# One-hot products of the first expert pair in half tiles among the router's steps, and the first pair's order of work, in a hybrid retention / attention / MoE block

## The chip, the cores and the metric

The kernel runs on one core of a Trainium2 chip as one program. Times are device microseconds, from the first to the last instruction of an execution and a little around it; the metric is the median of several executions. One execution is taken with the hardware profiler, and all rows shown come from it.

## The reference

One decoder block on 512 tokens of width 1024, all float32:

```python
h = rms_norm(x, mix_norm_g);  z = h @ w_in                  # 1024 x 4864
y_r = (silu(rg) * group_norm(retention(rq, rk, rv))) @ w_ret_o
y_s = sliding_window_attention(rms(sq), rms(sk), sv) @ w_swa_o
x = x + (sigmoid(gate_r) * y_r + sigmoid(gate_s) * y_s) @ w_out
h = rms_norm(x, ffn_norm_g)
group = argmax(h @ w_rg + b_rg)                             # 4 groups
e1, e2 = top2(h @ w_re + b_re, inside the group)            # 8 experts in a group, 32 in all
x = x + sum over e1, e2 of  weight_e * (silu(h @ w_gate[e]) * (h @ w_up[e])) @ w_down[e]
x = x + sigmoid(rms_norm(x, ple_gate_norm_g) @ w_ple_gate) * rms_norm(p @ w_ple, ple_norm_g)
```

The experts' weights are 32 times 3 MB: gate and up together 2 MB, down 1 MB. They are read once.

## The kernel before

**Mixers.** Up to about 330 us the two mixers run. Then `wout(nh, t)` forms `x1 = x + merged @ w_out` for two halves of the columns and four token tiles t of 128, and the router's steps of tile t are laid among the products of later tiles by the lists `fill`.

**Router.** For a tile: `post_a` transposes x1 and sums its squares, `post_b` multiplies by the router's weights (bank 4), `post_t` is a chain of small VectorE steps that ends in the one-hot rows of the two chosen experts (L932 is its first one-hot sum), `post_c` counts each token's rank in its expert (TensorE, bank 6, L939; then `Rpf`, L944), `post_d` is a second chain of VectorE steps (weights of the two experts, one-hot row of the rank), `post_e` adds tokens and weights to the slot tables (TensorE, bank 7, L1008). `post_t` and `post_d` are generators: `turns(n)` sends n rounds of all that are open. Every engine works in the order in which the program names its instructions.

**Slots and pairs.** Each expert has 64 slots. Experts p and p + 16 form pair p, whose 128 slots are one tile. For pairs 1 to 15 the slots' tokens are fetched by an indirect DMA of GpSimd (`fetch`, L1053) from x1 in DRAM, with rows named by the table `toki`; TensorE turns them (`turn`, L1066) and VectorE multiplies by the norm's gain into `XG[p]` (`grow`, L951). Pair 0 has no fetch: `first(t)` forms the one-hot matrix `G0[t]` (L961) and multiplies x1 by it (L964, 16 products a tile), which sums to the turned tokens.

**A pair's work.** `gu` multiplies by gate and up (L1161, 32 products, the slots' weights freed after each half of the contraction), ScalarE takes silu (L1171) and VectorE multiplies (L1172); `ht` transposes twice (L1180) and copies (L1182); `down` has 16 products (L1203). Below pair 12 the result is scattered by token into the DRAM tensor `Y` (L1223). From pair 12 on, `combine` multiplies it by a one-hot matrix instead (L1232) and VectorE adds it to x2 (L1244, through three PSUM banks of the ring `gb`). `collect` reads Y back (L1444, eight reads of 0.5 MB) and `total` adds it (L1451, four adds after pair 13 and four after pair 14). `embed(t)` forms one tile of the per-layer embedding (L1263, then L1250 on ScalarE) at pairs 10 to 13. After pair 15 the tail (L1365 to L1424) follows.

**Weights.** SBUF is an arena of 101 units of 2 KB. A load of 1 MB takes a block of four units; there are 17 blocks for weights, and `AT` names a few places below unit 22 (`TZ`) for the first loads. `queue` lists all loads in a fixed order, for each pair gate/up (four loads) and then down (two); `pump` issues as many as there is room for on SyncE's queue (L315). `SyncE` also waits in order: a load waits until the last reader of its place is done. From pair 9 on, `KEEP` leaves units 46 to 73 out.

**Overflow.** `overflow()` treats experts with more than 64 tokens. It reads a count into registers of every engine and skips its body by a branch (`tc.If`, shown as L1280) when there is none, which is the case here. In the kernel before it stands in pair 0, between gate/up and the turning of pair 1.

Of the kernel before, what the change touches and what calls it, by code (L numbers as in the profile page):

```python
# [16 lines left out]
P = 128  # L17
# [167 lines left out]
def program(tc, I, out):  # L185
# [55 lines left out]
    AT = {("gu", 0, 0): 0, ("gu", 16, 0): 14, ("gu", 17, 1): 18}  # L241
# [51 lines left out]
    qi = [0]  # L293
# [584 lines left out]
    def post_a(t, hb):  # L878

        if hb == 0:  # L880
            XT[t] = (ar.get(4, at=4 + 2 * (t % 2)), small(2), small(1), small(1))
        xt, ss, ms, r = XT[t]
        xs = x1[t].f(1024)[:, hb * 512:(hb + 1) * 512]
        b = aux()
        for kk in range(4):
            T.transpose(b[:, kk * P:(kk + 1) * P], xs[:, kk * P:(kk + 1) * P], ident)
        A.activation(xt.f(2, 512)[:, hb, :], b, AF.Copy)
        A.activation(banks[5], xs, AF.Square, accum_out=ss[:, hb:hb + 1])

    def post_b(t, hb):  # L890
# [4 lines left out]
        if hb:  # L895
            xt.free()
# [61 lines left out]
    def first(t):  # L958

        g0 = G0[t].f(2, SLOTS)  # L960
        V.tensor_tensor(g0, C("io64")[:, None, :].to_broadcast([P, 2, SLOTS]),  # L961
                        Rpf[:, t, 0:2][:, :, None].to_broadcast([P, 2, SLOTS]), op=OP.is_equal)
        for k in range(8):
            T.matmul(banks[k // 4][:, (k % 4) * P:(k % 4 + 1) * P], x1[t].f(8, P)[:, k, :], G0[t].f(P),  # L964
                     start=(t == 0 and k % 4 == 0), stop=(t == 3), skip_group_check=True)
        if t == 3:
            XG[0] = ar.get(4, at=12)
            for hb in range(2):
                grow(hb, banks[hb], XG[0])
# [87 lines left out]
    def turn(p_, hb):  # L1057

        if p_ > 15:
            return  # L1060
        if hb == 0:
            XG[p_] = ar.get(4, at=12 + 2 * (p_ % 2))
        b = gb()
        for kk in range(4):
            k = hb * 4 + kk
            T.transpose(b[:, kk * P:(kk + 1) * P], XR[p_].f(8, P)[:, k, :], ident)  # L1066
        grow(hb, b, XG[p_])
        if hb:
            XR.pop(p_).free()
            fetch(p_ + 2)  # L1070
# [6 lines left out]
    es.enter_context(tc.manual_schedule(engines=MS))  # L1077
    for t in range(4):
# [11 lines left out]
    for t in range(4):  # L1090
# [27 lines left out]
        pump(1 if t == 3 else 0)  # L1118
    turns()
# [150 lines left out]
    def overflow():  # L1270

        gm, tb_, xg, h, th, o = (ar.get(kb, r=r, at=at) for kb, r, at in (
            (2, True, 1), (4, False, 2), (4, False, 8), (2, False, 4), (2, False, 5), (4, False, 6)))
        xr = ar.get(4, at=12)
        wb = [ar.get(8, at=14)] * 2
# [97 lines left out]
    tmain = Ring([1, 0, 6, 7])  # L1373
# [81 lines left out]
    for p_ in range(16):  # L1455
        if p_ in KEEP:
            ar.kept = set(range(*KEEP[p_]))
        if p_ == SC:
            collect()
        for lo in (0, 4):  # L1460
            pump(0)
            gu(p_, range(lo, lo + 4))
        pump(0)
        if p_ == 0:
            overflow()
            fetch(2)
        turn(p_ + 1, 0)
        turn(p_ + 1, 1)
# [8 lines left out]
        if p_ == SC - 1:  # L1477
            for i in range(8):
                V.tensor_scalar(io[:, i * SLOTS:(i + 1) * SLOTS], C("io64"), i * SLOTS - 1.0, None, op0=OP.add)
# [89 lines left out]
```

## Time and profile before

| what | value |
|---|---|
| median of 3 runs | 710.86 us (710.43 to 712.74) |
| the profiled execution's own time | 713.99 us |
| its span, first to last instruction | 712.2 us |
| TensorE busy | 657.6 us (92%) |
| VectorE, ScalarE, GpSimd busy | 45%, 28%, 9% |
| granted TensorE clock, mean | 0.977 |
| moved by DMA | 163.92 MB |

A line of the timeline gives start, duration, engine, source line, operation, out<-in, shape and count; instructions of a kind that follow each other are merged, so a merged line's duration runs from the first start to the last end. PE is TensorE, DVE VectorE, ACT ScalarE, POOL GpSimd, SP SyncE; a q behind the engine marks its sequencer. In square brackets stands how long the engine was idle before it and what ended that.

### The profile page before, as it was taken

To read this page: it belongs to the slowest core of one execution; us is meant where nothing else is said; L and a number is where in the kernel's file an instruction comes from. 1 tells how busy PE (TensorE), PEld (TensorE's weight loads), DVE (VectorE), ACT (ScalarE), POOL (GpSimd) and SP (SyncE) were. 2 spreads that over 40 slices of the span, in tenths; PEclk is the share of its full clock that TensorE was granted. 3 is DMA by queue.
4 is the path that set the end of the run, shared out by engine and by line. 5 is a ranking of instruction groups with operands and counts; after the bars stand their busy time and mean duration, and the time that the engine had idled before them with its cause. 6 is when DMAs were issued, how large, how long until landed. Compare 5 with 4: busy or idle time off the path is not lost. (4 is left out here: it accounts for less than half of the span.)

```text
span 712.2 us, 8327 instructions
## 1 busy us (share of the span) xinstructions
PE 657.6 (92%) x3194; PEld 447.5 (63%) x3194; DVE 317.1 (45%) x692; ACT 198.2 (28%) x390; POOL 66.9 (9%) x67
## 2 busy tenths in 40 slices
PE   7999999999999999999988498998878889898997
PEld 6868887878888888888884243333323334334786
DVE  5485545842466156442362112112112234677753
ACT  6654243543334334230420000000001111006231
POOL 2013000000010000000000111111101121005100
PEclk9999999999999999999999799999999999999999
DMA  9727211340335420339891399999999989990011
GB/s 279 279 80 285 80 60 60 118 178 1 119 119 228 186 100 19 119 130 422 335 368 61 148 395 422 418 419 421 418 422 418 391 358 417 420 390 4 30 44 45
DMA packets 32474, 163.92 MB, mean 230 GB/s; under 512 B 5344, under 2 KB 8032, under 8 KB 16304
## 3 DMA queue, kind: packets, MB, share of 16 engines
q1 hardware_dynamic: 26672, 149.90, 53.2%
q0 software_dynamic: 5040, 11.35, 4.1%
q10 hardware_dynamic: 720, 2.11, 0.7%
q8 instruction: 26, 0.43, 0.3%
q14 instruction: 16, 0.13, 0.0%
HBM read 155.67 MB, written 14.68 MB: 239 GB/s over the span
## 5 line engine op out<-in xcount | busy, mean ns | idle before, releaser
L422 PE MATMUL bank<-slab,slab 128*128 128x512 f32 x320 | 126.4, 395 | 0.0
L423 PE MATMUL bank<-slab,slab 128*128 128x512 f32 x320 | 125.0, 391 | 0.0
L424 PE MATMUL bank<-slab,slab 128*128 128x512 f32 x320 | 124.8, 391 | 0.0
L1161 PE MATMUL bank<-slab,slab 128*64 128x512 f32 x512 | 118.7, 607 | 4.2 <-DMA slab<-wgu 4.2
L1161 PEld LDWEIGHTS bank<-slab,slab 128*64 128x64 f32 x512 | 43.5, 140 | 75.9 <-issue 67.7
L1203 PE MATMUL bank<-slab,slab 128*64 128x512 f32 x256 | 62.6, 631 | 27.3 <-DVE slab L1182 13.0
L339 DVE TENSOR_TENSOR slab<-slab,slab 128x1024 fp32r<-128x1024 f32 (+2 forms) x50 | 53.9, 1092 | 57.1 <-ACT slab L338 42.3
L422 PEld LDWEIGHTS bank<-slab,slab 128*128 128x128 f32 x320 | 60.1, 188 | 14.0 <-issue 1.8
L424 PEld LDWEIGHTS bank<-slab,slab 128*128 128x128 f32 x320 | 60.1, 188 | 12.7
L423 PEld LDWEIGHTS bank<-slab,slab 128*128 128x128 f32 x320 | 60.2, 188 | 11.7
L338 ACT ACTIVATE slab<-slab 128x1024 fp32r<-128x1024 f32 (+2 forms) x50 | 46.3, 952 | 56.4 <-PE bank L423 25.1
L1203 PEld LDWEIGHTS bank<-slab,slab 128*64 128x64 f32 x256 | 21.2, 144 | 58.0 <-issue 46.9
L1172 DVE SCALAR_TENSOR_TENSOR slab<-slab,st,bank 128x256 f32<-128x256 f32 x16 | 7.7, 480 | 104.5 <-ACT slab L1171 104.5
L1413 PE MATMUL bank<-slab,slab 128*128 128x512 f32 (+1 forms) x216 | 47.6, 376 | 3.3 <-DVE slab L1367 1.6
L1413 PEld LDWEIGHTS bank<-slab,slab 128*128 128x128 f32 x216 | 37.7, 193 | 11.9 <-DVE slab L1367 2.5
L1171 ACT ACTIVATE slab<-bank,st 128x256 f32<-128x256 f32 x16 | 7.6, 474 | 131.1 <-PE bank L1161 131.1
L1216 DVE COPY slab<-bank 128x512 f32<-128x512 f32 x12 | 8.3, 692 | 49.8 <-PE bank L1203 43.6
L870 PE MATMUL bank<-slab,slab 128*128 128x512 f32 x64 | 26.1, 408 | 0.0
L951 DVE TENSOR_TENSOR slab<-bank,vec 128x512 f32<-128x512 f32 x32 | 20.6, 683 | 11.0 <-SPq L1280 7.6
L872 PE MATMUL bank<-slab,slab 128*128 128x512 f32 x64 | 25.0, 391 | 0.0
L871 PE MATMUL bank<-slab,slab 128*128 128x512 f32 x64 | 24.9, 390 | 0.0
L1053 POOL DMA_INDIRECT slab<-X,st x15 | 15.5, 1032 | 99.3 <-PE bank L1066 66.3
(234 smaller groups left out, 873.6 us busy)
## 6 DMA issues: line engine op xcount, KB each, us to landing
slab<-wgu SPq DMA_DIRECT2D x64, 1024.0 KB, 18.3
slab<-wd SPq DMA_DIRECT2D x31, 1024.0 KB, 15.3
slab<-win SPq DMA_DIRECT2D x17, 1024.0 KB, 5.7
slab<-x SPq DMA_DIRECT2D x8, 512.0 KB, 3.5
Y<-slab SPq DMA_DIRECT2D x8, 512.0 KB, 5.1
slab<-wout SPq DMA_DIRECT2D x4, 1024.0 KB
slab<-Y POOLq DMA_DIRECT2D x8, 512.0 KB
slab<-wpg SPq DMA_DIRECT2D x4, 1024.0 KB, 9.5
```

What stands on the lines that cost most here:

```text
L338: A.activation(H.r(*shape), rawap, AF.Copy)
L339: (eng or V).tensor_tensor(L.r(*shape), rawap, H.f(*shape), op=OP.subtract)
L422: T.matmul(ps, wh[:, k, :], hh[k], start=(k == 0), stop=False)
L423: T.matmul(ps, wh[:, k, :], hl[k], start=False, stop=False)
L424: T.matmul(ps, wl[:, k, :], hh[k], start=False, stop=(k == nk - 1))
L870: T.matmul(ps, a, wh[:, kk, :], start=(k == 0), stop=False)
L871: T.matmul(ps, a, wl[:, kk, :], start=False, stop=False)
L872: T.matmul(ps, b, wh[:, kk, :], start=False, stop=(k == 7))
L951: V.tensor_tensor(xg.f(2, 4, P)[:, hb], b.rearrange("p (k i) -> p k i", k=4), gain[:, 4 * hb:4 * hb + 4][:, :, None].to_broadcast([P, 4, P ...
L1161: T.matmul(b[j * 64:(j + 1) * 64, :], xg[:, k, j * 64:(j + 1) * 64], load(("gu", p_ + 16 * j, k // 4)).f(4, 512)[:, k % 4, :], start=(k == ...
L1203: T.matmul(bs[nh][j * 64:(j + 1) * 64, :], t.f(2, P)[:, f, j * 64:(j + 1) * 64], load(("wd", p_ + 16 * j)).f(2, 1024)[:, f, nh * 512:(nh + ...
L1413: T.matmul(b, (H, L, H)[i][:, k, :], w, start=(k, i) == terms[0], stop=(k, i) == terms[-1])
```

## The change

Seven things are changed.

1. `first(t)` is split into `first0(t)` (the one-hot matrix) and `first(t, hb)` (eight of the 16 products, one PSUM bank). The parts are placed among the router's last steps; `post_t(3)` is sent as a whole, and `post_d(2)`, `post_d(3)` are sent in parts around it.
2. Pair 0's gate/up begins before the slot tables: two of eight contraction steps, then `post_e(2)`, `post_e(3)`, `tables()` and the fetches of pairs 1 and 2, then the rest. `counts()` follows gate/up.
3. Other loads have the low places: gate/up halves (0, 1) at unit 0, (16, 1) at unit 4, (1, 0) at 14, (17, 1) at 18. (16, 1) is `LATE`: it leaves the queue until the router's transposed tiles (`XS`, units 4 to 7) are free, and is then put in next. A low place no longer needs a free block.
4. `overflow()` stands at the start of pair 12, with its tiles at units 58 to 73.
5. `combine(p - 1)` of pairs 13 to 15 stands ahead of gate/up of pair p; before, it stood behind it.
6. In a pair, the two turning halves are transposed first, then `ht`, then the gain multiplications (`turned`), then `embed`, then `down`.
7. Y is read by ScalarE's queue in pair 12 ahead of `down`, and no longer by GpSimd's at the start of pair 12. The rings of banks change: gate/up 5 and 0, `gb` 2, 3 and 1, the tail 0, 6 and 7.

```diff
-    AT = {("gu", 0, 0): 0, ("gu", 16, 0): 14, ("gu", 17, 1): 18}
+    AT = {("gu", 0, 1): 0, ("gu", 16, 1): 4, ("gu", 1, 0): 14, ("gu", 17, 1): 18}
+    LATE = (("gu", 16, 1),)
...
+        for item in late[:]:
+            if not any(ar.used[item[3]:item[3] + item[2] // 2]):
+                late.remove(item)
+                queue.insert(qi[0], item)
...
+            if key in LATE and any(ar.used[at:at + kb // 2]):
+                late.append(queue.pop(qi[0]))
+                continue
...
-            if len(ar.blocks()) < reserve + (kb > 4) or at is not None and any(ar.used[at:at + kb // 2]):
+            low = at is not None and at < ar.TZ
+            if not low and len(ar.blocks()) < reserve + (kb > 4) or at is not None and any(ar.used[at:at + kb // 2]):
                 return
...
-            fill[3] += [w1free, call(turns), call(post_c, 1)]
+            fill[3] += [w1free, call(turns), call(post_c, 1), call(first0, 0), call(first0, 1)]
...
+    first(0, 0)
     turns()
     post_a(3, 1)
     post_h(3)
     pump(0)
     post_c(2)
+    first(0, 1)
     post_e(1)
+    first0(2)
+    chains.append(post_d(2))
+    turns(3)
     post_b(3, 1)
-    for t in range(2):
-        first(t)
-    chains.extend((post_t(3), post_d(2)))
+    first(1, 0)
+    first(1, 1)
+    pump(0)
+    for _ in post_t(3):
+        pass
+    first(2, 0)
+    post_c(3)
+    first0(3)
     turns()
-    first(2)
-    post_c(3)
-    post_e(2)
-    first(3)
     chains.append(post_d(3))
+    turns(4)
+    first(2, 1)
+    XG[0] = ar.get(4, at=12)
+    for hb in range(2):
+        first(3, hb)
+        grow(hb, banks[hb], XG[0])
     turns()
-    post_e(3)
-    tables()
-    for t in range(4):
-        G0[t].free()
-    gb = Ring([2, 3, 5])
-    fetch(1)
-    counts()
-    pump(0)
-    main = Ring([0, 1])
+    main = Ring([5, 0])
+    gb = Ring([2, 3, 1])
...
-                G.dma_start(y.f(1024), Y[i * S + t * P:i * S + (t + 1) * P, :])
+                A.dma_start(y.f(1024), Y[i * S + t * P:i * S + (t + 1) * P, :])
...
         if p_ == SC:
-            collect()
-        for lo in (0, 4):
-            pump(0)
-            gu(p_, range(lo, lo + 4))
+            overflow()
...
+        if p_ > SC:
+            for t in range(4):
+                combine(p_ - 1, t)
         pump(0)
         if p_ == 0:
-            overflow()
-            fetch(2)
-        turn(p_ + 1, 0)
-        turn(p_ + 1, 1)
+            gu(0, range(2))
+            post_e(2), post_e(3)
+            for t in range(4):
+                G0[t].free()
+            tables()
+            fetch(1), fetch(2)
+            gu(0, range(2, 4))
+        else:
+            gu(p_, range(4))
+        pump(0)
+        gu(p_, range(4, 8))
+        pump(0)
+        if p_ == 0:
+            counts()
+        bs = turn(p_ + 1)
+        ht(p_)
+        turned(p_ + 1, bs)
         for t in range(4):
             if PU[t] == p_:
                 embed(t)
-        if p_ > SC:
-            for t in range(4):
-                combine(p_ - 1, t)
-        ht(p_)
+        if p_ == SC:
+            collect()
         down(p_)
```

## Rows read from the trace of the kernel before

**Rows 1.** Windows: engines' busy time, granted clock, DMA share, GB/s.

```profile
375.00:385.00 10.00, 7.13 (x59) 5.32 (x59) 5.26 (x29) 1.55 (x4) 0.51 (x1) 0.91 0.07 29
...
375.00:415.00 40.00, 28.08 (x143) 13.90 (x141) 8.05 (x34) 2.84 (x6) 4.22 (x4) 0.83 0.35 127
415.00:540.00 125.00, 109.87 (x518) 45.39 (x518) 24.31 (x45) 9.64 (x18) 18.21 (x18) 0.99 1.02 420
...
560.00:575.00 15.00, 12.90 (x49) 5.41 (x49) 5.26 (x17) 1.99 (x6) 2.65 (x3) 0.89 0.79 314
575.00:638.00 63.00, 55.31 (x239) 23.17 (x236) 34.03 (x53) 7.85 (x18) 6.45 (x11) 1.00 1.02 417
```

**Rows 2.** Timeline, end of the router and pair 0.

```profile
369.36 7.23 PE L964 MATMUL bank<-slab,slab 128*128 128x128 f32 x48
...
373.27 0.19 DVE L932 TENSOR_TENSOR slab<-slab 128x32 f32<-128x32 f32 x1
...
376.57 0.39 PE L939 MATMUL bank<-slab,ct 128*128 128x32 f32 x2
...
379.65 0.69 DVE L951 TENSOR_TENSOR slab<-bank,vec 128x512 f32<-128x512 f32 x1 [0.20 <-PE bank L964]
...
382.17 0.72 PE L1008 MATMUL bank<-slab,slab 128*64 128x48 f32 x8 [2.55 <-DVE slab L999]
...
383.16 8.76 PE L1161 MATMUL bank<-slab,slab 128*64 128x512 f32 x32
...
400.56 1.29 DVE L951 TENSOR_TENSOR slab<-bank,vec 128x512 f32<-128x512 f32 x2 [7.57 <-SPq L1280]
...
402.28 6.05 PE L1203 MATMUL bank<-slab,slab 128*64 128x512 f32 x16 [7.11 <-DVE slab L1182]
...
408.10 7.09 PE L1161 MATMUL bank<-slab,slab 128*64 128x512 f32 x32
```

**Rows 3.** Timeline, an undisturbed pair behind its gate/up.

```profile
428.34 1.09 PE L1066 MATMUL bank<-ct,slab 128*128 128x128 f32 x8
...
430.56 0.41 DVE L1182 COPY slab<-bank 128x256 f32<-128x256 f32 x1
431.12 3.65 PE L1203 MATMUL bank<-slab,slab 128*64 128x512 f32 x16 [1.18 <-DVE slab L1182]
```

**Rows 4.** Timeline, TensorE's wait in pair 9.

```profile
522.51 5.34 PE L1161 MATMUL bank<-slab,slab 128*64 128x512 f32 x14 [2.09 <-DMA slab<-wgu]
```

**Rows 5.** Timeline, pair 10, the first with an embedding tile.

```profile
542.07 1.09 PE L1066 MATMUL bank<-ct,slab 128*128 128x128 f32 x8
...
543.00 3.60 PE L1263 MATMUL bank<-slab,slab 128*128 128x512 f32 x8
...
548.92 3.65 PE L1203 MATMUL bank<-slab,slab 128*64 128x512 f32 x16 [2.10 <-ACT bank L1250]
```

**Rows 6.** Timeline, pairs 14 and 15.

```profile
620.13 1.09 PE L1066 MATMUL bank<-ct,slab 128*128 128x128 f32 x8 [2.37 <-DMA slab<-X,st]
...
632.24 4.87 DVE L1451 TENSOR_TENSOR slab<-slab,slab 128x1024 f32<-128x1024 f32 x4
...
638.81 4.86 DVE L1244 TENSOR_TENSOR slab<-slab,bank 128x512 f32<-128x512 f32 x8
...
644.06 3.65 PE L1203 MATMUL bank<-slab,slab 128*64 128x512 f32 x16 [1.17 <-DVE slab L1182]
...
648.39 0.69 DVE L1214 TENSOR_TENSOR slab<-bank,slab 128x512 fp32r<-128x512 f32 x1 [1.03 <-ACT slab L1213]
```

**Rows 7.** The chain that ended last: start, us, what.

```profile
573.10 8.75 DMA Y<-slab,st
...
591.35 28.74 DMA slab<-X,st
```

**Rows 8.** Lines L1280 (383 to 401 us) and L315 (330 to 660 us).

```profile
L1280 SPq EVENT_SEMAPHORE  x9: 17/17/17, 393.9 to 400.4; - x9
...
DMA to landing us min/median/max: 5.5/15.9/23.4
```

More of the change, by code (lines that the diff above doesn't have):

```diff
@@ L291, in program @@
         want(("wpg", i), I["wpg"][i], 8)
-    qi = [0]
+    qi, late = [0], []
     def pump(reserve, until=None):
+        for item in late[:]:
+            if not any(ar.used[item[3]:item[3] + item[2] // 2]):
+                late.remove(item)
+                queue.insert(qi[0], item)
         while qi[0] < len(queue) and until not in loaded:
             key, src, kb, at = queue[qi[0]]
+            if key in LATE and any(ar.used[at:at + kb // 2]):
+                late.append(queue.pop(qi[0]))
+                continue
             if key == ("tables",):
@@ L895, in post_b @@
         if hb:
-            xt.free()
+            if t > 1:
+                xt.free()
             V.tensor_scalar(ms, ss[:, 0:1], ss[:, 1:2], EPS * D, op0=OP.add, op1=OP.add)
@@ L956, in post_h, with first0, first @@
         A.dma_start(X1[t * P:(t + 1) * P, :], x1[t].f(1024))
-    def first(t):
-        g0 = G0[t].f(2, SLOTS)
-        V.tensor_tensor(g0, C("io64")[:, None, :].to_broadcast([P, 2, SLOTS]),
+    def first0(t):
+        V.tensor_tensor(G0[t].f(2, SLOTS), C("io64")[:, None, :].to_broadcast([P, 2, SLOTS]),
                         Rpf[:, t, 0:2][:, :, None].to_broadcast([P, 2, SLOTS]), op=OP.is_equal)
-        for k in range(8):
-            T.matmul(banks[k // 4][:, (k % 4) * P:(k % 4 + 1) * P], x1[t].f(8, P)[:, k, :], G0[t].f(P),
+    def first(t, hb):
+        for k in range(4 * hb, 4 * hb + 4):
+            T.matmul(banks[hb][:, (k % 4) * P:(k % 4 + 1) * P], x1[t].f(8, P)[:, k, :], G0[t].f(P),
                      start=(t == 0 and k % 4 == 0), stop=(t == 3), skip_group_check=True)
[L966 to L969, printed above, removed]
     def oh(t):
@@ L1055, in fetch, with turn, turned @@
                              bounds_check=S - 1, oob_is_err=False)
-    def turn(p_, hb):
+    def turn(p_):
+        if p_ > 15:
+            return ()
+        bs = [gb(), gb()]
+        for hb in range(2):
+            for kk in range(4):
+                T.transpose(bs[hb][:, kk * P:(kk + 1) * P], XR[p_].f(8, P)[:, 4 * hb + kk, :], ident)
+        XR.pop(p_).free()
+        fetch(p_ + 2)
+        return bs
+    def turned(p_, bs):
         if p_ > 15:
             return
[L1061 to L1070, printed above, removed]
+        XG[p_] = ar.get(4, at=6 if p_ == 1 else 12 + 2 * (p_ % 2))
+        for hb in range(2):
+            grow(hb, bs[hb], XG[p_])
     def call(f, *a):
@@ L1077, in program @@
     es.enter_context(tc.manual_schedule(engines=MS))
+    XS = [ar.get(4, at=4), ar.get(4, at=6)]
     for t in range(4):
@@ L1123, in program @@
     post_c(2)
+    first(0, 1)
     post_e(1)
+    first0(2)
+    chains.append(post_d(2))
+    turns(3)
     post_b(3, 1)
-    for t in range(2):
-        first(t)
-    chains.extend((post_t(3), post_d(2)))
+    first(1, 0)
[6 more added lines that the diff above has]
+    first0(3)
     turns()
-    first(2)
-    post_c(3)
-    post_e(2)
-    first(3)
     chains.append(post_d(3))
-    turns()
-    post_e(3)
-    tables()
-    for t in range(4):
-        G0[t].free()
-    gb = Ring([2, 3, 5])
-    fetch(1)
-    counts()
-    pump(0)
-    main = Ring([0, 1])
+    turns(4)
+    first(2, 1)
+    XG[0] = ar.get(4, at=12)
+    for hb in range(2):
+        first(3, hb)
+        grow(hb, banks[hb], XG[0])
+    turns()
+    main = Ring([5, 0])
+    gb = Ring([2, 3, 1])
     tbk = Ring([4])
@@ L1272, in overflow @@
         gm, tb_, xg, h, th, o = (ar.get(kb, r=r, at=at) for kb, r, at in (
-            (2, True, 1), (4, False, 2), (4, False, 8), (2, False, 4), (2, False, 5), (4, False, 6)))
-        xr = ar.get(4, at=12)
-        wb = [ar.get(8, at=14)] * 2
+            (2, True, 58), (4, False, 60), (4, False, 62), (2, False, 59), (2, False, 64), (4, False, 66)))
+        xr = ar.get(4, at=68)
+        wb = [ar.get(8, at=70)] * 2
         count = lambda ap: nc.values_load(ap, min_val=0, max_val=S, skip_runtime_bounds_check_because=(
@@ L1372, in program @@
     aux = Ring([4, 5])
-    tmain = Ring([1, 0, 6, 7])
+    tmain = Ring([0, 6, 7])
     HL, RN, OO, TB = {}, {}, {}, {}
@@ L1458, in program @@
         if p_ == SC:
-            collect()
-        for lo in (0, 4):
-            pump(0)
-            gu(p_, range(lo, lo + 4))
+            overflow()
+            for i in range(8):
+                V.tensor_scalar(io[:, i * SLOTS:(i + 1) * SLOTS], C("io64"), i * SLOTS - 1.0, None, op0=OP.add)
+        if p_ > SC:
+            for t in range(4):
+                combine(p_ - 1, t)
         pump(0)
         if p_ == 0:
-            overflow()
-            fetch(2)
-        turn(p_ + 1, 0)
-        turn(p_ + 1, 1)
+            gu(0, range(2))
[15 more added lines that the diff above has]
+        turned(p_ + 1, bs)
         for t in range(4):
```

5 lines of the change are left out of this document (1 added, 4 removed).

## The prediction

> **What bounds the kernel now.** I read the stretches first. From 415 to 575 us and again from 575 to 638 us the DMA engines are full or nearly so [rows 1]: the weights stream at 420 GB/s, so that 1 MB takes 2.5 us. Ahead of that, from 375 to 415 us, their share is 0.35: they stand idle for 40 x 0.65 = 26.0 us. All 17 blocks are then loaded, and a new load can start only when TensorE has used up a block. So the transfers of the whole expert stage wait for the start of pair 0.
>
> The timeline of that stretch shows why pair 0 is late [rows 2]. The last tile's chosen experts are known at 373.27 + 0.19 = 373.46, but TensorE counts them at 376.57, since 48 one-hot products (7.23 us, 0.15 each) stand ahead in its queue. Then follow, one behind the other, 16 more products, the gain (to 380.34), the second VectorE chain, the slot tables and, at 383.16, gate/up. That takes 8.76 us where the next pair's takes 7.09; in 375 to 415 the granted clock was 0.83 on the mean, a mixture of its two levels, 2.4 and 1.2 GHz. Gate/up ends at 391.92 and down starts at 402.28, 10.4 us later; in an undisturbed pair it is 431.12 - 428.34 = 2.8 us [rows 3]. The difference, 7.6 us, is the skipped overflow branch: VectorE waits 7.57 us for SyncE at L1280, where SyncE leaves its last wait at 400.4 [rows 2, 8].
>
> Later, in pairs 9 and 10, TensorE waits for weights [rows 4]: what the transfers gain in 375 to 415 arrives there. From pair 11 on TensorE's own order and VectorE's adds set the pace; the waits that end last there name VectorE, ScalarE and once a gather [rows 5, 6].
>
> **The first pair.** Of the 64 one-hot products, 16 now fall ahead of `post_b(3)`, where about half of their 2.4 us fills waits, so that it ends 1.1 us later than the 369.36 of before, about 370.5. Twenty-four more (3.6 us) bring TensorE to the count at 374.1, just behind the chain, and this to 374.6. VectorE then has two short steps (0.5), the rest of tile 2's second chain and four steps of tile 3's. One such chain takes some 2.2 us, by the stretch from 380.34 to a little behind 382.17 [rows 2]; about 2.5 for these parts, and 0.69 for the first gain: gate/up starts at about 378.3, 4.9 us earlier. A quarter takes 7.09/4 = 1.8; the slot products wait for the chain's end (about 380.4) and end at 380.9; so the first half of the weights is free at 382.7, and gate/up ends at 386.2. The fetch of pair 1 goes out right behind the tables, with more than half of gate/up still to come, so I count no wait for it. Down follows after 2.8 - 0.6 us (next part) and ends at 392.0. Pair 1 starts there instead of at 408.10, 16 us earlier, of which 7.6 are the branch.
>
> **What the transfers gain.** Before, data ended about 0.7 us behind 375 (0.07 of 10 us [rows 1]). One more load fits (unit 4): to 378.2. I take 1 us from a place's release to data. Idle to 383.7: 5.5 us. Two blocks (5.0) and three fetches (0.5 MB with empty slots, half of 1.25 us, say 0.7 each) last to 390.8; idle to 393.0: 2.2. Down's two blocks, a scatter and one block from each half of pair 1 (the other two stand below unit 22 and give no room), with a fetch, last to 404.4; idle until pair 1's down ends: 1.4. From there loads wait for the DMA. Idle in all 9.1 against 26.0: the gain is **16.9 us**. Bounds: 12 if pair 0 meets the slow clock and a late fetch (4 us more of idle, and 1), 18 if the last gap closes.
>
> **An ordinary pair.** `ht` no longer stands behind the gain multiplications (1.28 us of VectorE): down starts after turning 1.09, two transposes and a copy of 0.41 with their hand-overs, 2.2 instead of 2.8. The 0.6 us in pairs 1 to 9 are worth nothing: they end in the wait for weights [rows 4], which hides them; without it they would be 5 us.
>
> **Pairs 10 to 15.** From the end of pair 10's gate/up to the last product of pair 15's down it is 644.06 + 3.65 - 542.07 = 105.6 us now [rows 5, 6]. Afterwards, with gate/up 7.1 and 5.6 from its end to the next start (2.2 plus 3.4 of down):
> - with an embedding tile (pairs 10 to 13) 8.7 instead of 5.6, since its 3.6 us fill the wait for the copy and down no longer waits behind ScalarE's squares [rows 5]: 8.7 for pair 10, 15.8 for pair 11.
> - Pair 12: the branch. I take 2 us for each engine's read, jump and hand-over; bounds 0 (hidden behind weights) and 7.6. SyncE must let its loads land first, but what VectorE waited for at pair 0 was a place that the branch's loads also use; at units 58 to 73 only Y's reads follow. 17.8.
> - Pair 13: `combine` ahead of gate/up needs the second half of the split result, 1.4 us behind down (648.39 + 0.69 - 647.71), then five of eight adds (4.86/8 = 0.61 each) before the last bank is free, and 0.9 of products: 5.4. With 15.8: 21.2.
> - Pairs 14, 15: between split and adds VectorE now runs `total`, 4.87 us [rows 6], which gate/up covered before. Above, the adds waited for nothing; here 9.9. Pair 14: 9.9 + 7.1 + 5.6 = 22.6; pair 15, with no turning to fill silu: 22.8. If the adds were hidden, both would be some 9 us less together; that is the lower bound.
>
> Sum 108.9: **3.3 us lost**. `io`'s eight short steps and eight issues on ScalarE hide behind the products of pair 12. The tail stays; three banks instead of four suffice for one eviction per 24 products.
>
> **Reads of Y.** On GpSimd's queue they delay the fetch behind them: it took 28.74 us, and TensorE waited 2.37 for it [rows 6, 7]. On ScalarE's queue they wait for the last scatter (8.75 us [rows 7]), which was issued some 14 us earlier; behind them stands the copy of pair 12's down, about 1 us. The 2.37 are left out of my sum for pair 14. The Trainium skill, DMA: Bandwidth & Descriptors, "Issuing engines are not separate DMA queues", says that DMAs of all engines interleave on the same 16 and that another issuer saves only issue time. By that rule the fetch would stay late and the result be 2.4 us longer; that the fetch stands behind the reads in their own queue speaks against it here.
>
> **Sum.** -16.9 + 3.3 = -13.6. Against the profiled execution 713.99 - 13.6 = 700.4; that one lay 3.1 above the median, so **697.3** for the median.
>
> **Rivals.** A measurement here can tell 0.3%, 2.1 us.
> - *The transfers set the end* (17%): if they, not TensorE, pace pairs 11 to 15, the new order costs nothing and the 3.1 us of idle in 560 to 575 go as well: 710.86 - 16.9 - 3.1 = 690.9. For it: share 1.02 in 575 to 638; against it: no late wait of TensorE names weights.
> - *The branch costs 7.6 at pair 12 too* (16%): 702.9.
> - *Pair 0 stands for its last load* (9%): gate/up (16, 1) goes out only after `post_b(3)`. Landing at 392 instead of some 380, it would make pair 0 9 us later: gain 8, 706.2. Against it: DMA is idle then.
> - *Slower* (8%): at pair 12 SyncE has a full queue, where at pair 0 it had the two loads for which gate/up's second half had made room. A load takes 15.9 us to land, at most 23.4 [rows 8]. Should the engines stand until all have landed, the branch costs between these, 19.6 say, 17.6 more than I took: 714.9. It decides from 15.6 us on. For it: VectorE did wait for SyncE; against it: after the branch no compute engine uses those places soon. The Trainium skill, Runtime: NRT & Kernel Launch, "Instruction fetch mechanics", adds that a taken branch out of the two pages in store must fetch by DMA first. No row here shows such a fetch behind a full queue; it would lengthen this case.
>
> Likeliest: 50%. Its own range, from gain 12 to 18 and branch 0 to 7.6, is 694 to 708. The range to 707 from 690 takes in all but the slower case and tails. Faster by over 0.3%: 86%; within: 5%, from the ends of the last two cases; slower: 9%.
>
> **What would show it.** In the profile after: gate/up of pair 0 near 378 and pair 1 near 392; DMA idle 9 us between 375 and 415; pair 10's gate/up ends near 525; waits at L1280 in pair 12, and whom they name; TensorE waits some 4 us longer at L1232 in pairs 14 and 15, on L1244 behind L1451; the fetch of pair 15 lands within its pair. Wrong would be: idle DMA behind 406, waits on weights in pairs 13 to 15, or TensorE standing over 8 us at the branch.

## The result, and the profile after

The changed kernel takes 730.75 us (median of 4 runs, 729.17 to 731.07), the kernel before on the same chip 710.64 (709.75 to 712.74): the ratio is 1.0274, with an interval of 1.0247 to 1.0301. It is 20 us slower, where 13.6 us faster was forecast, and lies outside the range of 690 to 707 that the forecast gives. The profiled execution took 731.07 us, 17.1 more than that of before, with a span of 729.3.

The stretches of [rows 1] in the kernel after (columns: stretch; its length; busy time of TensorE, its weight loads, VectorE, ScalarE and GpSimd with instructions; granted clock; DMA share; GB/s):

```profile
375.00:385.00 10.00, 7.89 (x50) 3.41 (x50) 3.25 (x17) 1.59 (x2) 2.20 (x2) 1.00 0.56 224
375.00:415.00 40.00, 33.60 (x162) 15.02 (x164) 9.28 (x30) 3.42 (x5) 6.23 (x6) 0.91 0.64 243
415.00:540.00 125.00, 112.95 (x508) 46.40 (x506) 26.73 (x49) 11.01 (x22) 17.75 (x18) 0.96 1.02 420
560.00:575.00 15.00, 13.26 (x58) 4.85 (x54) 4.24 (x9) 1.85 (x5) 1.74 (x2) 1.00 0.50 183
575.00:638.00 63.00, 38.98 (x148) 18.57 (x150) 24.62 (x38) 4.60 (x10) 0.72 (x1) 0.76 0.79 317
```

In 375 to 415 DMA stands idle for 40 x 0.36 = 14.4 us, against 26.0: 11.6 us are won. From 560 on they are lost again. TensorE's timeline up to 415 us, to be set against [rows 2]:

```profile
375.77 1.94 PE L1180 MATMUL bank<-slab,slab 128*64 128x512 f32 x8 [0.96 <-issue]
377.51 0.65 PE L1016 MATMUL bank<-slab,slab 128*64 128x48 f32 x16
377.96 5.36 PE L1180 MATMUL bank<-slab,slab 128*64 128x512 f32 x24
...
388.15 1.97 PE L1072 MATMUL bank<-ct,slab 128*128 128x128 f32 x8 [4.49 <-DMA slab<-X,st]
...
391.06 5.63 PE L1222 MATMUL bank<-slab,slab 128*64 128x512 f32 x16 [0.52 <-DVE slab L1201]
396.48 7.07 PE L1180 MATMUL bank<-slab,slab 128*64 128x512 f32 x32
```

Gate/up of pair 0 (L1180) begins at 375.77, but the turning of pair 1 (L1072) then waits 4.49 us for its fetch, and down (L1222) takes 5.63 us where it takes 3.65 in an undisturbed pair. Pair 1 starts at 396.48 instead of 408.10. The later pairs, against [rows 5, 6]:

```profile
530.78 1.09 PE L1072 MATMUL bank<-ct,slab 128*128 128x128 f32 x8
...
557.69 7.09 PE L1180 MATMUL bank<-slab,slab 128*64 128x512 f32 x32 [1.44 <-DVEq L1299]
...
569.75 3.65 PE L1222 MATMUL bank<-slab,slab 128*64 128x512 f32 x16
593.56 6.99 PE L1251 MATMUL bank<-slab,slab 128*128 128x512 f32 x16 [20.16 <-ACT slab L1232]
600.48 7.09 PE L1180 MATMUL bank<-slab,slab 128*64 128x512 f32 x32
...
622.98 4.46 PE L1251 MATMUL bank<-slab,slab 128*128 128x512 f32 x10 [4.42 <-DVE slab L1263]
...
660.60 5.35 PE L1222 MATMUL bank<-slab,slab 128*64 128x512 f32 x16 [0.52 <-DVE slab L1201]
```

The row at 593.56 is the result: TensorE stands for 20.16 us until ScalarE has made the first half of pair 12's split (L1232). ScalarE's own timeline shows why ScalarE was late:

```profile
570.80 0.34 ACTq L1463 DMA_DIRECT2D slab<-Y  x1
571.07 0.19 ACT L1269 ACTIVATION_READ_ACCUMULATOR bank<-bank 128x1 f32 x1
571.47 21.40 ACTq L1463 DMA_DIRECT2D slab<-Y  x7
592.91 1.09 ACT L1232 ACTIVATE slab<-bank 128x512 fp32r<-128x512 f32 x2 [21.64 <-DMA slab<-wgu]
```

Issuing the eight reads of Y takes from 570.80 to 592.86, and the wait of the copy behind them is put down not to a read, but to a load of weights from SyncE's queue. The single issues say more. The fourth starts at 580.73, and a load of SyncE landed at 580.71; the seventh starts at 592.05, and another landed at 592.03. A completion semaphore is a counter that a transfer raises when it has landed. In the trace's records of waits, each of the eight issues waits on the semaphore that its own transfer will raise, and these are among the eight that SyncE's loads raise and wait on: loads and reads take turns on the same completion semaphores, and an issue waits until the transfer that used its semaphore last has landed.

The books, in the profiled executions: up to the end of pair 10's gate/up 11.3 us are won (530.78 against 542.07); from there to the end of pair 15's down 665.95 - 530.78 = 135.2 us pass, against 105.6, so 29.6 are lost; 1.1 are won in the tail. That makes 17.2 lost in all, and 17.1 was measured. Of the 11.3 us, 1.8 don't belong to the change: the first product of `wout`, in work that it leaves alone, already starts at 308.54 instead of 310.37. Counted from there, 9.5 us are won up to pair 10's gate/up, and the whole takes 18.9 longer, close to the 20.1 of the medians.

### The profile page after: what moved, and what is told of

It reads as the page before. It is cut to its first block, busy times and chain, and to the rows that moved or that the text cites. A ratio compares the mean times of both kernels' runs of the same rounds, so it can differ in the third digit from the quotient of the medians.

```text
span 729.3 us, 8326 instructions
## 1 busy us (share of the span) xinstructions
PE 662.7 (91%) x3194; PEld 448.3 (61%) x3194; DVE 320.5 (44%) x692; ACT 197.7 (27%) x390; POOL 62.6 (9%) x59
## 5 line engine op out<-in xcount | busy, mean ns | idle before, releaser
L1180 PE MATMUL bank<-slab,slab 128*64 128x512 f32 x512 | 120.8, 607 | 9.6 <-DMA slab<-wgu 7.2
L431 PE MATMUL bank<-slab,slab 128*128 128x512 f32 x320 | 126.4, 395 | 0.0
L432 PE MATMUL bank<-slab,slab 128*128 128x512 f32 x320 | 124.9, 390 | 0.0
L433 PE MATMUL bank<-slab,slab 128*128 128x512 f32 x320 | 124.8, 391 | 0.0
L1180 PEld LDWEIGHTS bank<-slab,slab 128*64 128x64 f32 x512 | 42.6, 139 | 82.9 <-issue 71.5
L431 PEld LDWEIGHTS bank<-slab,slab 128*128 128x128 f32 x320 | 60.1, 188 | 14.0 <-issue 1.8
L1222 PE MATMUL bank<-slab,slab 128*64 128x512 f32 x256 | 62.4, 628 | 6.6 <-issue 5.1
L433 PEld LDWEIGHTS bank<-slab,slab 128*128 128x128 f32 x320 | 60.1, 188 | 12.7 <-DVE slab L348 0.2
L432 PEld LDWEIGHTS bank<-slab,slab 128*128 128x128 f32 x320 | 60.2, 188 | 11.7
L1251 PE MATMUL bank<-slab,slab 128*128 128x512 f32 x64 | 25.3, 536 | 29.8 <-ACT slab L1232 20.2
L1190 ACT ACTIVATE slab<-bank,st 128x256 f32<-128x256 f32 x16 | 7.6, 474 | 161.4 <-PE bank L1180 161.4
L1222 PEld LDWEIGHTS bank<-slab,slab 128*64 128x64 f32 x256 | 20.5, 143 | 40.5 <-issue 35.6
L1432 PEld LDWEIGHTS bank<-slab,slab 128*128 128x128 f32 x216 | 36.8, 189 | 12.2 <-DVE slab L1386 2.5
L1251 PEld LDWEIGHTS bank<-slab,slab 128*128 128x128 f32 x64 | 16.0, 263 | 39.9 <-ACT slab L1232 22.5
L879 PE MATMUL bank<-slab,slab 128*128 128x512 f32 x64 | 26.1, 408 | 0.0
L881 PE MATMUL bank<-slab,slab 128*128 128x512 f32 x64 | 25.0, 391 | 0.0
L880 PE MATMUL bank<-slab,slab 128*128 128x512 f32 x64 | 24.9, 390 | 0.0
## 6 DMA issues: line engine op xcount, KB each, us to landing
slab<-wd SPq DMA_DIRECT2D x31, 1024.0 KB, 17.1
```

Of the source, the lines that this page charges most:

```text
L431: T.matmul(ps, wh[:, k, :], hh[k], start=(k == 0), stop=False)
L432: T.matmul(ps, wh[:, k, :], hl[k], start=False, stop=False)
L433: T.matmul(ps, wl[:, k, :], hh[k], start=False, stop=(k == nk - 1))
L879: T.matmul(ps, a, wh[:, kk, :], start=(k == 0), stop=False)
L880: T.matmul(ps, a, wl[:, kk, :], start=False, stop=False)
L881: T.matmul(ps, b, wh[:, kk, :], start=False, stop=(k == 7))
```

## Experiments

"Repaired" below means the changed kernel with the reads of Y on GpSimd's queue and `combine` behind gate/up. Kernels were timed beside the kernel before; where two were not on the same chip, their ratios are compared.

### 1. The reads of Y

```diff
-                A.dma_start(y.f(1024), Y[i * S + t * P:i * S + (t + 1) * P, :])
+                G.dma_start(y.f(1024), Y[i * S + t * P:i * S + (t + 1) * P, :])
```

> The changed kernel with one thing undone: the eight reads of Y go out on GpSimd's queue again, at the same place in pair 12. Theory 1 (each of ScalarE's read issues waits until the load of SyncE that last used the same completion semaphore has landed, and ScalarE, which works in order, brings pair 12's split copy late): the 20.16 us that TensorE waits at the first combine of pair 13 go, and the time falls by 18 to 21 us, to 710 to 713. Theory 2 (the reads wait for their places, for the last scatter or for their share of the transfers, whoever issues them): the split copy is early, but then the adds of Y or the loads are as late as now; the time falls by less than 5 us. If GpSimd's fetches stand behind the reads, a fetch wait of some 2 us comes back in pair 14 or 15.

708.58 us, ratio 0.9927 (0.9895 to 0.996). TensorE's timeline at the same place:

```profile
570.44 3.65 PE L1222 MATMUL bank<-slab,slab 128*64 128x512 f32 x16
574.03 1.29 PE L1251 MATMUL bank<-slab,slab 128*128 128x512 f32 x3
575.55 3.81 PE L1251 MATMUL bank<-slab,slab 128*128 128x512 f32 x13 [0.23 <-DVE slab L1233]
579.28 7.09 PE L1180 MATMUL bank<-slab,slab 128*64 128x512 f32 x32
```

The 20.16 us are gone and the time with them: 22 us by the medians, 25 by the ratios. The reads themselves are no faster (8.4 to 32.4 us from issue to landing, against 8.2 to 9.4 on ScalarE's queue), but nobody stands behind them; and in the records they use eight other semaphores, which no load of SyncE raises. So what cost the time was the waiting issuer, not the traffic of Y. TensorE waits for no fetch either: the fetch for which it waited in pair 14 [rows 6] is issued ahead of the reads in this order.

The same reads, still on ScalarE's queue, but directly behind the branch:

```diff
             overflow()
+            collect()
...
-        if p_ == SC:
-            collect()
         down(p_)
```

> The changed kernel with the reads of Y still on ScalarE's queue, but directly behind the overflow branch at the start of pair 12, where SyncE's loads have all landed and its next ones are not yet issued. Theory 1 (ScalarE's issues wait for SyncE's loads on shared completion semaphores): no load is under way that they could wait for, the eight issues take about 0.7 us each from the landing of the last scatter on, the wait of 20.16 us at the first combine of pair 13 goes, and the time falls by 14 to 21 us; SyncE's next loads now wait for the reads on those semaphores, some us. Theory 2 (reading on ScalarE's queue is slow by itself, or the places or the scatter hold it): the issues again take some 20 us, silu of pair 12 stands behind them, and the time stays within 5 us of the changed kernel's.

728.0 us, ratio 1.0221 (1.0176 to 1.0267): not what was expected. ScalarE leaves the branch at 553.35, long ahead of SyncE:

```profile
566.99 13.16 ACTq L1463 DMA_DIRECT2D slab<-Y  x8
580.20 0.47 ACT L1190 ACTIVATE slab<-bank,st 128x256 f32<-128x256 f32 x1 [27.42 <-DMA slab<-Y]
```

The last of SyncE's loads lands at 566.46, the first read goes out at 566.99. In the records SyncE, as it leaves the branch, raises that read's semaphore at 566.73, and ScalarE goes on at 566.75. My premise was wrong that nothing would be under way: ScalarE only waits earlier, and now silu (L1190) stands behind it. Inside the 13.16 us, the sixth read goes out at 572.00 when the first landed at 571.98: reads wait for reads, too.

To see whether the branch has a part in it, `overflow()` was left out of the changed kernel (reads on ScalarE's queue):

```diff
-            overflow()
```

> The changed kernel, reads of Y on ScalarE's queue ahead of pair 12's down, without the overflow branch (the treatment of experts with more than 64 tokens is left out). Theory 1 (each read's issue waits for SyncE's load that last used its completion semaphore): the branch has no part in it, SyncE even has more loads under way when the reads come; the eight issues again take 15 us or more, TensorE waits 15 to 22 us at the first combine of pair 13, and the time is 722 to 732. Rival (ScalarE is held by the branch: its reads use places that the skipped body uses too, and so wait for SyncE to leave it): the wait at the first combine goes, and the time falls to 705 to 713.

717.68 us, ratio 1.0074 (1.0044 to 1.0105): between the two ranges that were expected.

```profile
569.18 10.97 ACTq L1463 DMA_DIRECT2D slab<-Y  x7
580.20 1.08 ACT L1232 ACTIVATE slab<-bank 128x512 fp32r<-128x512 f32 x2 [10.86 <-DMA slab<-Y]
```

The wait stays without a branch, so the branch alone isn't its cause, but about half of its length goes: TensorE waits 9.38 us. Here six reads go out within 3 us and the seventh at 579.34, after the second's landing at 579.32. With the branch, SyncE comes out of it at 568.8 and issues six loads within 3 us just as the reads come, and they share the semaphores with these.

The part alone, in the kernel before (same edit on L1444, G to A):

> The kernel before with one thing changed: the eight reads of Y go out on ScalarE's queue, where they stand at the start of pair 12. Theory 1 (shared completion semaphores): SyncE has its loads under way there, each read's issue waits for a load's landing, silu of pair 12 comes after them, and the time grows by 8 to 20 us. Theory 2 (what costs is the place ahead of the split, or what the branch just ahead of it leaves behind): here neither exists, and the time stays within 2 us; the fetch wait of 2.37 us in pair 14 goes in either case.

722.24 us, ratio 1.0122 (1.0081 to 1.0162), 8.7 us slower. The size fits theory 1, but the trace gives another reason for most of it. ScalarE's silu waits 16.0 us for the reads,

```profile
ACT slab L1171 <- DMA slab<-Y: 16.0, 1, 16.0
```

and the first read goes out at 582.03, when the last scatter landed at 582.01. At that place the reads wait for the scatter first; only the seventh, at 587.55, waits for another landing (the second read's, at 587.53). What is common to the four runs is this: whatever a DMA issue waits for, ScalarE's next instruction waits for as well.

### 2. `combine` behind gate/up, and the branch at pair 12

```diff
-        if p_ > SC:
-            for t in range(4):
-                combine(p_ - 1, t)
         pump(0)
...
         if p_ == SC:
             collect()
+        if p_ > SC:
+            for t in range(4):
+                combine(p_ - 1, t)
         down(p_)
```

> The changed kernel with the reads of Y on GpSimd's queue, and with combine of pairs 13 to 15 again behind the gate/up and the turning of the next pair instead of ahead of gate/up. Theory 5 (TensorE waits for the banks of combine since the adds of Y stand between split and adds on VectorE, two waits of 4.42 us, and again for the first split): the waits at combine fall below 1 us each, and the time is 8 to 11 us shorter than with the reads on GpSimd's queue alone, near 702. Rival (late transfers pace pairs 13 to 15, since SyncE stood at the branch from 549 to 569): the same us turn up as waits for weights, and the two kernels differ by less than 3 us.

698.88 us, ratio 0.9814 (0.9769 to 0.9858), 9.7 us below the reads on GpSimd's queue alone. The waits of 4.42 us are gone; some of the gain is spent on waits for weights in pairs 13 and 14, as the rival had it in kind:

```profile
572.29 3.80 PE L1180 MATMUL bank<-slab,slab 128*64 128x512 f32 x16 [0.60 <-DMA slab<-wgu]
578.72 3.65 PE L1180 MATMUL bank<-slab,slab 128*64 128x512 f32 x14 [2.64 <-DMA slab<-wgu]
...
602.60 3.65 PE L1180 MATMUL bank<-slab,slab 128*64 128x512 f32 x14 [1.63 <-DMA slab<-wgu]
```

The repaired kernel without `overflow()`:

> The changed kernel with the reads of Y on GpSimd's queue, combine behind gate/up, and without the overflow branch (the treatment of experts with more than 64 tokens is left out). With the branch SyncE issues no load for some 20 us in pair 12, the share of DMA is 0.57 in 560 to 575 us, and TensorE waits 0.60 + 2.64 + 1.63 = 4.9 us for weights in pairs 13 and 14 and 1.4 at the branch. Theory A (the branch costs by SyncE's stop): these waits go, and the time falls by 4 to 7 us against the 698.9 with the branch, to 692 to 695. Theory B (the loads have no free places there anyway, and were late in the kernel before too, whose share was 0.79): the time falls by less than 2.5 us. The slower rival of the prediction (compute engines stand until all loads have landed, 17 us and more) would show as 15 us.

693.82 us, ratio 0.9736 (0.9703 to 0.9769): the branch costs 5 us at pair 12. The stretch from 560 to 575 us with the branch and without it; the DMA share, last but one, is 0.57 and 1.02:

```profile
560.00:575.00 15.00, 14.25 (x61) 5.26 (x58) 5.63 (x11) 3.04 (x7) 5.98 (x10) 1.00 0.57 220
```

```profile
560.00:575.00 15.00, 14.88 (x64) 5.70 (x60) 5.63 (x11) 3.05 (x7) 6.01 (x10) 1.00 1.02 421
```

TensorE loses 1.4 us at the branch itself; its waits for weights in pairs 13 and 14 are 4.9 us with the branch and 2.2 without. Together that is 4.1 of the 5 us. The second part I put down to SyncE, which issues nothing in the branch until its loads have landed. In the kernel after, SyncE waits 19.6 us there, for nobody but itself:

```profile
SPq L1299 <- SPq L1299: 19.6, 2, 19.1
```

### 3. The branch at pair 0, in the kernel before

```diff
         if p_ == 0:
-            overflow()
             fetch(2)
```

> The kernel before without the overflow branch (the treatment of experts with more than 64 tokens is left out). It tests the term of 7.6 us in the prediction. If the branch is what holds pair 0's down, pair 1's gate/up starts 6 to 8 us earlier, near 401, idle time of DMA between 375 and 415 us falls from 27 us to about 20, and the time falls by 5 to 8 us, to 704 to 708. Rival (without it pair 0 waits for the fetch of pair 1 or for the slow clock instead): the time falls by less than 3 us.

699.98 us, ratio 0.9834 (0.9798 to 0.9869): 12 us, more than the 7.6 of the prediction. TensorE's timeline:

```profile
381.00 7.09 PE L1161 MATMUL bank<-slab,slab 128*64 128x512 f32 x32
388.02 1.09 PE L1066 MATMUL bank<-ct,slab 128*128 128x128 f32 x8
...
394.22 7.11 PE L1161 MATMUL bank<-slab,slab 128*64 128x512 f32 x32
```

From gate/up of pair 0 to that of pair 1 it is 13.2 us, against 24.9 in [rows 2], 11.7 less. Of these, 7.7 lie between gate/up and down. There VectorE's wait is gone, and with it TensorE's at the branch, which in the kernel before was this:

```profile
393.86 1.09 PE L1066 MATMUL bank<-ct,slab 128*128 128x128 f32 x8 [1.94 <-DVEq L1280]
```

The other 4.0 are the clock: gate/up takes 7.09 us instead of 8.76 and down 3.72 instead of 6.05, and the granted clock of 375 to 415 us is 1.00. Gate/up runs ahead of the branch, so it is not shown that the branch slows it. In the six profiled kernels with the branch in pair 0 that gate/up took 8.3 to 9.5 us; in this one and the one without a branch in section 4 it took 7.09.

Two ways to take VectorE's wait away and keep the branch. First other places: pair 1's tokens (units 14 and 15) and silu's transposed result (unit 2) no longer lie where SyncE's loads of the skipped body would write.

```diff
-            (2, True, 1), (4, False, 2), (4, False, 8), (2, False, 4), (2, False, 5), (4, False, 6)))
-        xr = ar.get(4, at=12)
+            (2, True, 1), (4, False, 12), (4, False, 4), (2, False, 8), (2, False, 9), (4, False, 2)))
+        xr = ar.get(4, at=6)
...
-            XG[p_] = ar.get(4, at=12 + 2 * (p_ % 2))
+            XG[p_] = ar.get(4, at=4 if p_ == 1 else 12 + 2 * (p_ % 2))
...
-            o = ar.get(4, at=4 + 2 * (p_ % 2))
+            o = ar.get(4, at=6 - 2 * (p_ % 2))
```

> The kernel before with other places alone: the overflow branch stays in pair 0, but the tokens of pair 1 (units 14 and 15 before) and silu's transposed result (unit 2) no longer lie where SyncE's loads of the skipped body would write. Theory P (at pair 0 VectorE waits 7.6 us only since these places have SyncE as their last writer, and SyncE reaches the end of the branch when its loads have landed): the 7.1 and 1.9 us of waits at pair 0 fall below 3 in all, pair 1's gate/up starts 6 to 9 us earlier, and the time falls by 6 to 12 us, to 701 to 707; without the branch at all it fell by 12.8. Rival (all engines meet at the branch whatever the places): less than 2 us.

702.04 us, ratio 0.9875 (0.9837 to 0.9913). Second, the branch ahead of the loads:

```diff
-        pump(0)
         if p_ == 0:
             overflow()
+        pump(0)
+        if p_ == 0:
             fetch(2)
```

> The kernel before with one pair of steps exchanged: in pair 0 the overflow branch comes ahead of the issue of loads instead of behind it; its places are as before. Theory P (VectorE waits 7.6 us because SyncE reaches the end of the branch only when the two loads that it issued just ahead have landed): SyncE has nothing under way there, the 7.1 us wait at pair 0 falls below 1, and the time falls by 7 to 12 us, to 701 to 706. Rival (the branch costs by itself, by its read, jump and fetch of instructions): less than 3 us.

704.35 us (699.5 to 708.47), ratio 0.9896 (0.9852 to 0.9939). VectorE's wait of 7.57 us at L951 [rows 2] in the one and in the other:

```profile
392.88 1.29 DVE L951 TENSOR_TENSOR slab<-bank,vec 128x512 f32<-128x512 f32 x2 [1.56 <-PE bank L1066]
```

```profile
394.93 0.69 DVE L951 TENSOR_TENSOR slab<-bank,vec 128x512 f32<-128x512 f32 x1 [1.76 <-PE bank L1066]
```

Both take it away. In the first, SyncE still stands at the branch until 398.7, but VectorE no longer needs its places and goes on without it; in the second, SyncE has nothing under way there and is through at 385.3. What is left is TensorE's wait of 1.93 us at the branch, in both, and the slow clock: in the second, the profiled execution was granted 0.83 in 375 to 415 us, gate/up of pair 0 took 9.51 us and down 5.80.

### 4. The first pair and the order within a pair

The kernel before, without the branch, with the changed order within a pair alone (turning, `ht`, gain, `embed`, `combine`, `down`):

> The kernel before without the overflow branch (left out) and with the changed kernel's order within a pair alone: both turning halves, then the transposes of silu's result, the gain multiplications, the embedding, combine, down. The changed kernel without the branch, with the reads of Y on GpSimd's queue and combine behind gate/up, took 693.8, the kernel before without the branch 700.0. Theory H (the reordered router end and the early start of pair 0 win nothing, since pair 1's fetch lands no earlier for TensorE; the 6.2 us between the two come from the order within a pair): 692.5 to 695.5. Rival (the head wins some us): 696 to 700.

693.6 us, ratio 0.9761 (0.972 to 0.9803). The repaired kernel without the branch, which has the whole new router end as well, took 693.82 (0.9736): the two differ by 0.2 us in the medians and 1.8 in the ratios, so the half tiles and the early start of pair 0 win next to nothing. Counted from the first product of `wout`, gate/up of pair 0 starts 4.8 us earlier with them (67.2 against 72.0 us), but pair 1's 2.4 us later (87.0 against 84.6), since its fetch takes longer. Against the same kernel in the old order (699.98) the order within a pair wins 6.4 us, 5.2 by the ratios. In the profiles 3.9 of it lie between the end of pair 10's gate/up and the end of pair 15's down, 105.3 us in the old order and 101.5 in the new.

Two edits of the repaired kernel were to hold back the two loads that go out beside that fetch: the first issue of loads in pair 0 left out, and all gate/up places given back only behind the last product.

> The changed kernel with the reads of Y on GpSimd's queue and combine behind gate/up, and in pair 0 without the issue of loads that stands right behind the first half of gate/up, so that the fetches of pairs 1 and 2 find the DMA engines empty and the two loads go out behind gate/up's second half. Theory 6 (the fetch of pair 1 lands after 8.9 us, because its packets share the DMA engines with two loads of 1 MB): it lands after some 4 us, the 5.0 us that TensorE waits at the turning of pair 1 fall below 1.5, gate/up of pair 1 starts near 392 instead of 396, and the time falls by 1 to 4 us, less than the 4 to 5 at the head, since the two loads go out 3.5 us later. Rival (the fetch is slow by itself, by two fetches behind each other on GpSimd's queue): it still takes 7 us or more, and the time stays or grows by up to 3 us.

> The changed kernel with the reads of Y on GpSimd's queue and combine behind gate/up; in pair 0 all four gate/up loads are given back only after the last product, so that the two loads for which the first half made room cannot start at 380 us, when the fetches go out. Theory 6 (the fetch of pair 1 takes 8.9 us because it shares the DMA engines with those two loads): it lands some 4 us after its issue, near 384, TensorE's wait of 5.0 us at the turning of pair 1 falls below 1.5, gate/up of pair 1 starts near 391.5 instead of 396, idle time of DMA in 375 to 415 us falls by 1 to 4 us, and the time by as much, to 695 to 698. Rival (the fetch is slow by itself): it still takes 7 us or more, and the time grows by 1 to 4 us, since the loads go out later for nothing.

698.44 us (0.9797; 0.9763 to 0.9831) and 699.98 us (0.9825; 0.9799 to 0.9852). Neither edit did what it was made for: the first load went out at 381.29 and 381.62, 0.13 us behind the fetch as without the edit, and the fetch took 8.5 and 8.7 us. SyncE waits for the last reader of a place, wherever in the program the place is given back. So the readers themselves were reordered (the flag that ends pair 0's sums moves along with them):

```diff
-            gu(0, range(2, 4))
-        else:
-            gu(p_, range(4))
-        pump(0)
-        gu(p_, range(4, 8))
+            gu(0, (4, 5, 6, 7, 2, 3))
+        else:
+            gu(p_, range(4))
+            pump(0)
+            gu(p_, range(4, 8))
```

> The changed kernel with the reads of Y on GpSimd's queue and combine behind gate/up; pair 0's gate/up multiplies the contraction steps in the order 0, 1, 4 to 7, 2, 3, so that the places with room for new loads are read last and the two loads cannot go out at 380 us beside the fetches. Theory 6 (pair 1's fetch takes 8.9 us because its packets share the DMA engines with these two loads): it lands some 4 us after its issue, near 384, TensorE's wait of 5.0 us at the turning of pair 1 falls below 1.5, gate/up of pair 1 starts near 391.5 instead of 396, and the time falls by 0 to 3 us from 698.9, less than at the head, since the loads go out 3 us later. Rival (the fetch is slow by itself): it still takes 7 us or more, and the time grows by 1 to 3 us.

695.08 us (694.19 to 695.54), ratio 0.9772 (0.9742 to 0.9803). Its stretch 375 to 415 us, TensorE's rows, and the issue of pair 1's fetch (the last number is us to landing), which has no load beside it now:

```profile
375.00:415.00 40.00, 35.88 (x191) 16.71 (x189) 11.84 (x45) 4.38 (x9) 7.04 (x7) 1.00 0.79 298
```

```profile
386.60 1.07 PE L1072 MATMUL bank<-ct,slab 128*128 128x128 f32 x8
...
393.27 7.11 PE L1180 MATMUL bank<-slab,slab 128*64 128x512 f32 x32
```

```profile
slab<-X,st POOLq DMA_INDIRECT x1, 4.2
```

The fetch lands in 4.2 us instead of 8.9, no one waits for it, DMA stands idle for 40 x 0.21 = 8.4 us, and pair 1 starts at 393.27. This version is 15 to 16 us faster than the kernel before, 3 to 4 faster than the repaired kernel, and the best that has the branch. Counted from the first product of `wout`, pair 10's gate/up ends 16.2 us earlier than before.

Places, the branch ahead of the loads and the order within a pair were also put into the kernel before together, first without and then with the exchange of branch and loads:

> The kernel before with the branch in pair 0 and its places moved, and with the changed kernel's order within a pair (turning, silu's transposes, gain, embedding, combine, down). By theory P and theory H together: 694 to 700, 4 to 7 us below the version with the places alone, and at or below the 698.9 of the changed kernel with two of its parts undone. Rival (pairs 10 to 15 are paced by transfers, so that the order wins nothing once pair 0 is early): within 2 us of the version with the places alone.

> The kernel before with the branch in pair 0 ahead of the issue of loads, its places moved, and the changed kernel's order within a pair. Without any branch this order took 693.6. Theory P: what is left of the branch is the read, jump and hand-over, 2 to 3 us at pair 0 (TensorE waits 1.9 there), so 695 to 698, below the 698.9 of the changed kernel with two parts undone. Rival (the branch also delays pair 0's fetches and slows the clock, so that moving SyncE's part wins nothing): 699 to 701, as with the places alone.

700.4 us (0.9832; 0.9801 to 0.9863) and 699.27 us (0.9837; 0.9799 to 0.9875). The order brought 1.6 us over the places alone, as its rival had it, and emptying SyncE's queue nothing beyond the noise. In the second, gate/up of pair 0 took 9.50 us at a granted clock of 0.87; the branch at pair 0 stays dearer than the 2 to 3 us that I expected.

## Why the prediction was wrong, by its steps

- **Reads of Y: the step that failed.** "On ScalarE's queue they wait for the last scatter (8.75 us [rows 7]), which was issued some 14 us earlier; behind them stands the copy of pair 12's down, about 1 us." That wait was over, as I said (the scatter landed at 565.88), but I counted no other: the 15.9 us that a load takes to land [rows 8] I set only against SyncE, and not against an issue that has to wait for such a load. The copy waited 21.64 us, TensorE 20.16. Behind that wait pair 13's `combine` took 6.99 us, with a granted clock of 0.76 in 575 to 638 us. Putting the reads back took 22 to 25 us off. The slower rival had the right cause in kind (an engine stands until SyncE's queue has landed) at the wrong place: at the branch TensorE waited 1.44 us. With the reads put back the kernel was 5 us faster than before (ratio 0.9927) and not 13.6; the terms below explain the rest.
- **The Trainium skill**, DMA: Bandwidth & Descriptors, "Issuing engines are not separate DMA queues", says that another issuer saves only issue time. These runs don't test that: the fetch wait of 2.37 us [rows 6] was gone with GpSimd's queue as well, since this order issues the fetch ahead of the reads. That another issuer can lose 20 us, by waiting in order for other engines' transfers, is in neither that rule nor the rows I used.
- **Gain of the first pair, 16.9: mis-sized, about 11.** DMA idle fell by 11.6 us; by the timelines it is 9.5 in this execution, counted from the first product of `wout`, and 10.7 to 12.4 in the five other runs that are the same up to there (sections 1 and 2). Gate/up came 5.6 us earlier so counted, where I said 4.9, but "I count no wait for it", for the fetch, was wrong by 4.49: two loads went out beside it. With the loads behind it, the idle time was 8.4 us, where I had 9.1, and the gain 16.2. As the kernel stood, nearly all of the head's gain is the branch's leaving: the kernel before without it gains 12.3 at the same place.
- **Branch at pair 12, 2 us:** right for the compute engines (1.44), wrong in all, 5 us, as SyncE's stop leaves DMA idle. At pair 0 leaving it out won 12 and not 7.6, some 4 of them by the clock. The Trainium skill, Runtime: NRT & Kernel Launch, "Instruction fetch mechanics", says that a taken branch must fetch its target by DMA where the target is not in store; with SyncE's loads under way these 1.44 us show no long wait of that kind.
- **Pairs 10 to 15, 3.3 us lost:** without the stall, in the first experiment, it was 644.66 - 531.82 = 112.8 against 105.6, so 7.2. Pair 10's 8.7 were 8.4 and pair 13's 5.4 were 5.3; pairs 14 and 15 took 11.2 each instead of 9.9 (my own parts, 5.4 and 4.87 for `total`, make 10.3), and pair 15's down ran at the low clock, 5.35 instead of 3.65. That VectorE runs `total` between split and adds was the right reason, and undoing it gave 9.7 (8 by the ratios).
- **An ordinary pair, nothing:** borne out. Of the two kernels without a branch, the one in the old order ends pair 10's gate/up 219.4 us after the first product of `wout`, the one in the new order 218.8.

What stays open: why the granted clock falls in pair 0 in some of these kernels and not in others, though TensorE's wait ahead of it, 2.55 or 2.56 us, is the same in both; and how much of the 20.16 us each shared semaphore holds. That loads and reads share them is read from the records of waits and from landings that fall together with issues to 0.02 us; no run took the sharing itself away, except by another queue. Nor did a run issue the reads from ScalarE behind the copy, which would also have spared the copy the wait.

## What to carry to other kernels

Before a transfer is moved to another engine's queue, ask what its issue can wait for, and what stands behind it on that engine: an issue here took 0.33 us only if its completion semaphore was free, so give such reads to an engine with no work due. A skipped branch was paid by the engine with the longest queue under way. TensorE waited 1.4 to 1.9 us at it, and VectorE waited long only where it wrote to places that the first engine would use in the skipped body. An early start wins no more than the next thing to arrive allows: here a fetch that takes 4 us alone and 9 beside two loads. And before two timelines are compared at a late place, compare them at one ahead of the change: here they were already 1.8 us apart.

## What the runs showed of the hardware that was not expected

- ScalarE's eight issues of 0.5 MB reads took 22.1 us beside SyncE's loads, 11.3 with no branch ahead, and GpSimd's eight, on semaphores that SyncE's loads do not use, 4.4 in the first experiment.
- A fetch by row indices took 4.1 to 4.2 us from issue to landing on empty DMA engines, with a second one 1.5 us behind it, and 8.4 to 8.9 with two loads of 1 MB issued right after it.
- SyncE's stop of 19.6 us at the branch left DMA idle for only 7.5 us in 560 to 575 (15 x 0.50), since the loads issued before went on landing until 568.
